# Two-layer decoder trunk on one core: the first three products run together, and each unit of the heads has its scores, turns and output next to each other ahead of one piece of fill

## The chip, the cores and the metric

The kernel runs on one core of one Trainium2 chip. The metric is the device time of one execution in microseconds (us); the time before is the median of three runs. A profiled execution of the same kernel gives the trace that all rows below come from.

The core's engines each work through a queue of their own, in order: TensorE (PE in the profile) does matmuls and transposes, VectorE (DVE), ScalarE (ACT) and GpSimd (POOL) do the elementwise work, and SyncE (SP) issues DMAs. Matmul results go to PSUM, in eight buffers of 512 fp32 columns.

## The reference, cut to what matters

One inference step of a two-layer decoder trunk for 544 tokens: one prompt of 512 and eight samples of 4 each. `D_MODEL` is 1024.

```python
def layer(x, ...):
    h = rmsnorm(x, g_mix)
    z = h @ w_in                       # one projection, split by columns
    u_pool, q_raw, kv_raw, nsa_gate, c_b, c_c, c_x, gate_pool, gate_nsa, gate_conv = split_columns(z)
    y_pool, pool_new = pool_mixer(u_pool, ...)    # windows 2, 4, 8, 16, then a small map
    y_nsa, kv_rows, win_new = nsa_mixer(...)      # compressed, selected and window attention, 8 heads of 64
    y_conv, conv_new = short_conv_mixer(c_b, c_c, c_x, conv_past, conv_w)
    merged = (sigmoid(gate_pool) * (y_pool @ w_br_pool)
              + sigmoid(gate_nsa) * (y_nsa @ w_br_nsa)
              + sigmoid(gate_conv) * (y_conv @ w_br_conv))
    x = x + merged @ w_out
    f, ffn_new = conv_ffn(rmsnorm(x, g_ffn), ...) # (silu(conv3(h @ W_a)) * (h @ W_b)) @ W_down
    return x + f, ...
```

`rmsnorm` divides by the root of the mean square over the 1024 features. After the second layer a final norm gives the two outputs. Everything is fp32.

## The kernel before

**Layout and products.** `x` lies with features on partitions: eight tiles of 128 features by 544 tokens. A product multiplies eight weight tiles of 128x128 into two halves of 272 tokens. Every fp32 operand is split into a high and a low part in the format fp32r, and `mm3` (L328 to L332) does three matmuls for one tile and half: high by high, high by low, low by high. So one half of a product is 24 matmuls of 272 columns. A weight comes by DMA (L312, tile `wr`), ACT casts its high part in two halves (L304, `wh`), and DVE, or POOL while the heads run, subtracts the low part (L305, `wl`).

**The order.** PE's order is written by hand: `emit` runs through a list of products and `pump(us)` asks it for so many microseconds of product matmuls. ACT's and SP's orders are by hand in `setup` only. All other orders (DVE and POOL everywhere, ACT and SP after `setup`) come from the scheduler that builds the program; it may put an instruction that was written later ahead of an earlier one. `later(n, f)` runs `f` when `n` ticks have passed, and a half of a product (or one compression product) ends with a tick.

**Norm rows.** The squares are summed over tiles by ACT and DVE into `acc`. `rstd_sum` has PE sum over partitions (L381, tile `po`), and then runs a chain of twelve small DVE instructions on 5 columns (L384 to L390; three Newton steps of three instructions each, tiles `nv`, `ni`, `ny`, `nt`). `rstd_rows` (L400) broadcasts the result along partitions by transposes, and ACT copies it out of PSUM (L402, L403). The evacuations of the products that follow multiply by it (for instance L506 and L513).

**The start.** `setup` loads `x`, the constants and the first weights. In `emit` the first three products of a norm are special: the first two run together over seven tiles, then over the eighth, and the third one comes after; for the first norm the sum stands at its step 6 and the rows at its step 14 of 16. `setup` also loads cache pages (L486, tile `b`) and `begin` the layer's small tables.

**The projection stage.** A product of pooling inputs is followed, `pm` = 9 and 10 ticks later, by `pool_map` for its two halves: a matmul into a score buffer (L713, tile `ps`), ACT's scaled cast (L714) and DVE's low part (L715). Two groups of 16 tiles make the compressed keys and values: `cmp_split` splits the page rows with eight ACT casts (L566) and eight DVE subtractions (L568), and two compression products (L1383 to L1385) use them. The scores' tag has two PSUM buffers (`PS`), the turns' tag two (`PT`), products three (`G`), and sums and head outputs one (`PO`).

**The heads.** `attention` walks through 64 units a layer: 8 heads, two branches kk (0 selected, 1 window), four blocks b of 128 queries. In what follows S(kk,b) are the scores of a unit (L864), with DVE's causal add (L878), its negated maximum (L880), ACT's exponential (L886), DVE's reciprocal (L891) and POOL's scaling (L893, tile `P`). T(kk,b) is the turn of a unit, b+1 transposes on PE into one `PT` buffer (L906), evacuated by ACT (L908) and DVE (L909). C is the turn of the head's compressed scores (L930), which takes a `PT` buffer too (evacuated by L932 and L933). `head_out` (L939, L944) multiplies by the values. `head_q` makes the next head's scaled queries with two ACT instructions (L849) and two DVE instructions (L851, tile `Q`). Step u emits the scores of unit u, the turn of unit u-3, C when unit u-5 is (0,3), and outputs further back. Between these come pieces of fill, that is product matmuls (tile `pg`) which `yield self.fill / 2` (0.83 us each) asks for.

**The tail.** The last product writes the output tiles (`final_tile`, L1274 to L1285). Rows for the first half of the tokens come from one more chain, `final_rows` (L1295) multiplies by them, and `final_tokens` transposes the rest (L1307), sums `acc` and `side` (L381) and scales (L1318, L1319).

## Time and profile before

| what | value |
|---|---|
| median of three runs | 1736.14 us (1735.8 to 1737.05) |
| profiled execution: time, span | 1735.2 us, 1733.3 us |
| granted clock of the core, mean | 0.997 |
| PE busy | 1709.6 us (99% of the span), 13525 instructions |
| DVE, ACT, POOL busy | 1126.6, 740.4, 468.2 us |
| DMA | 175.52 MB, mean 101 GB/s |

The span is the stretch from the first to the last recorded instruction; 1.9 us lie around it. Busy time is summed over the whole span, so it says little of one stage: the timeline of a stretch shows what each engine did there, and the list of waits shows who stood still for whom. A row of a timeline gives the start and the length in us, the engine, the line of the program, the operation, the tiles as output<-inputs, shapes, the count of merged instructions and, in brackets, how long the engine had stood idle and what released it. PEclk is the granted clock of PE as a share of full speed. Matmuls overlap, so a row's length is longer than the distance from one to the next.

### The profile page before, as it was taken

How to read it: one execution, taken by the hardware profiler on the slowest of the kernel's cores; microseconds unless marked ns; L12 is line 12 of the kernel's file. 1: busy time of each engine (PE TensorE's matmuls, PEld its weight loads, DVE VectorE, ACT ScalarE, POOL GpSimd, SP SyncE). 2: the span in 40 equal slices, each digit the busy share in tenths (PEclk: the TensorE clock that was granted, in tenths of full speed). 3: DMA queues.
4: the chain of work that ended last, by engine and by line, in shares of the span. 5: the costliest groups of instructions: out<-in, count | busy, mean ns of one | idle time of the engine just before them, and what ended most of it. 6: DMA issues, size and time to landing. Idle time of an engine off the chain costs nothing.

```text
span 1733.3 us, 35135 instructions
## 1 busy us (share of the span) xinstructions
PE 1709.6 (99%) x13525; PEld 1689.0 (97%) x13525; DVE 1126.6 (65%) x2572; ACT 740.4 (43%) x1501; POOL 468.2 (27%) x692
## 2 busy tenths in 40 slices
PE   7999999999999999999999999999999999999998
PEld 7999999999999999999999899999999999999997
DVE  5675688756566565565757757877565665565666
ACT  4443566653333232233444436666443433232333
POOL 2412446630122121012034124566101321121120
PEclk9999999999999999999999999999999999999999
DMA  7546212235322322322455532212242222322322
GB/s 215 151 127 199 76 51 60 68 88 173 91 86 69 104 81 84 104 86 71 152 175 117 170 123 62 62 52 66 68 161 90 88 77 89 92 80 81 109 79 76
DMA packets 95976, 175.52 MB, mean 101 GB/s; under 512 B 30898, under 2 KB 49970, under 8 KB 95810
## 3 DMA queue, kind: packets, MB, share of 16 engines
q1 hardware_dynamic: 95666, 173.01, 33.4%
q8 instruction: 107, 1.75, 0.4%
q14 instruction: 59, 0.48, 0.1%
q10 hardware_dynamic: 144, 0.28, 0.1%
HBM read 157.19 MB, written 12.71 MB: 98 GB/s over the span
## 4 chain that ended last, share of the span: by engine, by line
PE 93%; DVE 2%; DMA 1%; ACT 1%; issue 1%; SPq 1%; POOL 1%; DVEq 0%; POOLq 0%; ACTq 0%
PE pg L329 27%; PE pg L330 27%; PE pg L332 27%; PE ps L864 2%; PE po L944 2%; PE pt L906 2%; DVE t L568 1%; PE ps L332 1%; PE ps L330 1%; PE ps L329 1%; DMA W<-W 1%; ACT b L566 1%; PE pt L930 0%; PE ps L1383 0%; PE po L381 0%
## 5 line engine op out<-in xcount | busy, mean ns | idle before, releaser
L329 PE MATMUL pg<-t,wh 128*128 128x272 f32 (+1 forms) x3808 | 1112.8, 293 | 2.1 <-ACT t L1260 1.4
L330 PE MATMUL pg<-t,wh 128*128 128x272 f32 (+1 forms) x3808 | 1095.6, 288 | 1.4 <-DVE t L1261 1.3
L332 PE MATMUL pg<-t,wl 128*128 128x272 f32 x3776 | 1086.5, 288 | 0.0
L329 PEld LDWEIGHTS pg<-t,wh 128*128 128x128 f32 (+1 forms) x3808 | 715.8, 188 | 6.7 <-ACT t L1260 2.0
L330 PEld LDWEIGHTS pg<-t,wh 128*128 128x128 f32 (+1 forms) x3808 | 716.0, 188 | 3.4 <-DVE t L1261 2.2
L332 PEld LDWEIGHTS pg<-t,wl 128*128 128x128 f32 x3776 | 711.0, 188 | 0.0
L304 ACT CAST wh<-wr 128x512 fp32r<-128x512 f32 (+2 forms) x524 | 313.3, 600 | 559.2 <-PE pg L330 438.7
L305 DVE TENSOR_TENSOR wl<-wr,wh 128x512 fp32r<-128x512 f32 (+2 forms) x428 | 290.7, 681 | 169.8 <-ACT wh L304 152.0
L1171 DVE TENSOR_TENSOR t<-t,pg 128x272 f32<-128x272 f32 x204 | 88.8, 436 | 92.8 <-PE pg L332 91.8
L1210 POOL TENSOR_TENSOR W<-W,W 128x512 f32<-128x512 f32 x44 | 77.9, 1770 | 229.2 <-ACT wh L304 190.3
L305 POOL TENSOR_TENSOR wl<-wr,wh 128x512 fp32r<-128x512 f32 (+1 forms) x96 | 113.2, 1183 | 35.9 <-ACT wh L304 33.6
L893 POOL TENSOR_SCALAR P<-P,ls,gate 128x128 f32<-128x128 f32 (+3 forms) x128 | 81.3, 635 | 121.3 <-DVE lc L920 43.2
L650 POOL COPY t<-W 128x2 f32<-128x2 f32 x44 | 10.8, 246 | 358.4 <-DVE W L1193 321.1
L348 DVE TENSOR_TENSOR t<-W,t 128x544 fp32r<-128x544 f32 x48 | 34.9, 727 | 78.5 <-ACT t L347 78.4
L886 ACT ACTIVATE P<-ps,mx 128x256 f32<-128x256 f32 (+1 forms) x144 | 71.7, 499 | 33.0 <-DVE mx L880 23.4
L908 ACT CAST b<-pt 128x128 fp32r<-128x128 f32 (+3 forms) x128 | 54.2, 423 | 71.4 <-PE pt L906 71.0
L909 DVE TENSOR_TENSOR b<-pt,b 128x128 fp32r<-128x128 f32 (+3 forms) x128 | 62.1, 485 | 10.3 <-ACT b L908 8.9
L347 ACT CAST t<-W 128x544 fp32r<-128x544 f32 x48 | 31.1, 647 | 82.8 <-POOL W L1211 78.2
L880 DVE TENSOR_REDUCE mx<-ps 128x1 f32<-128x256 f32 (+1 forms) x144 | 64.4, 447 | 1.6
L864 PE MATMUL ps<-t,Q 128*128 128x288 f32 (+6 forms) x288 | 62.5, 306 | 1.0 <-ACT P L886 0.7
L1200 ACT ACTIVATE W<-W 128x560 f32<-128x560 f32 x44 | 29.6, 673 | 74.8 <-DVE W L640 74.8
L369 POOL TENSOR_TENSOR t<-t,W 128x544 f32<-128x544 f32 x12 | 16.4, 1368 | 154.5 <-ACT W L360 154.5
(266 smaller groups left out, 1856.7 us busy)
## 6 DMA issues: line engine op xcount, KB each, us to landing
wr<-up SPq DMA_DIRECT2D x88, 512.0 KB, 3.6
wr<-w_in SPq DMA_DIRECT2D x82, 512.0 KB, 3.8
wr<-down SPq DMA_DIRECT2D x64, 256.0 KB, 2.7
wr<-w_out SPq DMA_DIRECT2D x16, 512.0 KB, 3.7
wr<-down SPq DMA_DIRECT2D x32, 192.0 KB, 2.4
b<-pgA SPq DMA_DIRECT2D x64, 64.0 KB, 2.5
wr<-cw SPq DMA_DIRECT2D x8, 512.0 KB, 4.7
wr<-br_a SPq DMA_DIRECT2D x32, 128.0 KB, 2.2
```

The source lines that it names most:

```text
L304: nc.scalar.copy(h, r[:, k0:k1])
L305: (eng or nc.vector).tensor_sub(w, r[:, k0:k1], h)
L329: self.nc.tensor.matmul(p[:m, :HF], wh, xh[:, cs], start=a, stop=False)
L330: self.nc.tensor.matmul(p[:m, :HF], wh, xl[:, cs], start=False, stop=b and wl is None)
L332: self.nc.tensor.matmul(p[:m, :HF], wl, xh[:, cs], start=False, stop=b)
L864: nc.tensor.matmul(p[:, :n], q[:, 128 * i:128 * i + 128], kd[:, c0:c0 + n], start=u == 0, stop=u == 1)
L880: nc.vector.tensor_reduce(mx[:, u:u + 1], p[:, c0:c0 + m], axis=AX.X, op=OP.max, negate=True)
L886: nc.scalar.activation(t[:, pos:pos + m], p[:, c0:c0 + m], AF.Exp, bias=mx[:, 0:1], accum_out=ls[:, u:u + 1])
L893: nc.gpsimd.tensor_scalar(t[:, 0:n], t[:, 0:n], ls[:, 0:1], self.gate[:, i, 1 + kk, hd:hd + 1], op0=OP.mult, op1=OP.mult)
L909: nc.vector.tensor_sub(blk(pt)[:, lo][:, ::-1], blk(p)[:, 0:i + 1], blk(pt)[:, hi])
L1171: self.halves(ps, lambda p, cs: nc.vector.tensor_add(self.x[m][:, cs], self.x[m][:, cs], p))
L1210: nc.gpsimd.tensor_mul(f[:, 0:NP], t[:, 0:NP], z[:, 0:NP])
```

## The change

The change touches five places.

1. **Start.** `setup` loads and splits the weights of three products, not two, in parts. For the first norm `emit` runs the three products together, tile by tile (six PSUM buffers), with the partition sum after the seventh tile and the rows after the eighth. Four pages move from `setup` into `begin`.
2. **Chain.** `rstd_sum` has one DVE instruction fewer (the shift by one is folded into a product with -0.5). A second accumulator goes through `token_sums` on its own and is added by one DVE instruction.
3. **Pool maps.** `pm` is 7 instead of 9.
4. **Heads.** `attention` collects the fill of a step and yields once, at its end.
5. **Other norms and tail.** In the other norms the sum comes ahead of the third product and the rows between its halves. In the tail the first `final_rows` come one tick later, two of the four after the last product.

```diff
-    def __init__(... pm=9, ...):
+    def __init__(... pm=7, ...):
...
+    def token_sums(self, p, acc, c0, n):
+        for j in range(-(-n // 128)):
+            t0 = c0 + min(128 * j, n - 128)
+            self.nc.tensor.matmul(p[:, j:j + 1], acc[:, t0:t0 + 128], self.ones[:, 0:1], start=True, stop=True)
+
-    def rstd_sum(self, acc, c0=0, n=NT):
+    def rstd_sum(self, acc, c0=0, n=NT, more=None):
...
+        self.token_sums(p, acc, c0, n)
         nc.vector.tensor_scalar(v, p[:, 0:nb], 1.0 / D, 1e-6, op0=OP.mult, op1=OP.add)
-        nc.vector.tensor_scalar(it, v.bitcast(I32), 1, None, op0=OP.logical_shift_right)
-        nc.vector.tensor_scalar(y.bitcast(I32), it, -1.0, float(0x5f3759df), op0=OP.mult, op1=OP.add)
+        if more is not None:
+            q = p[:, 8:8 + nb]
+            self.token_sums(q, more, c0, n)
+            nc.vector.scalar_tensor_tensor(v, q, 1.0 / D, v, op0=OP.mult, op1=OP.add)
+        nc.vector.tensor_scalar(y.bitcast(I32), v.bitcast(I32), -0.5, float(0x5f3759df), op0=OP.mult, op1=OP.add)
...
         norm(0)
-        part(0, 0, 2)
-        part(1, 0, 2)
+        for n in range(3):
+            part(n, 0, 2)
...
-        self.ahead(3)
...
         self.pages_cmp()
-        self.pages_some(0, range(0, 4))
...
-                yield self.fill / (1 if u < lag else 2)
+                us += self.fill / (1 if u < lag else 2)
             if 0 <= u - lag < len(units):
                 n, kk, b = units[u - lag]
                 self.head_turn(heads[n], kk, b)
-                yield self.fill / 2
+                us += self.fill / 2
             if 0 <= u - lag - 2 < len(units):
                 n, kk, b = units[u - lag - 2]
                 if (kk, b) == (0, 3):
                     self.head_cmp_turn(heads[n])
-                    yield self.fill / 2
+                    us += self.fill / 2
             for d, k1 in ((lag + 4, 0), (lag + 1, 1)):
                 if 0 <= u - d < len(units) and units[u - d][1:] == (k1, 3):
                     self.head_out(heads[units[u - d][0]], k1)
+            yield us
...
-                    for k in range(0, KT, 2):
-                        self.later(4 + k // 2, lambda k=k: self.final_rows(k))
+                    for k in (0, 2):
+                        self.later(5 + k // 2, lambda k=k: self.final_rows(k))
...
+        self.final_rows(4)
+        self.final_rows(6)
         turn(0, range(KT - 1))
-        y = self.rstd_sum([self.acc, self.side], HF, HF)
+        y = self.rstd_sum(self.acc, HF, HF, self.side)
...
+            if n == 0:
+                w3, rs = self.take(2), [self.G(), self.PT()]
+                for k in range(KT):
+                    for p, a, b in ((ps, w, t), (qs, w2, u), (rs, w3, v)):
+                        self.outer(p, a, x, [k], b.m)
+                    if k == KT - 2:
+                        y = self.rstd_sum(self.acc)
+                self.r = self.T()
+                self.rstd_rows(y, self.r)
...
```

Line numbers move by 0 to 8, so L851 is L853 after the change, L864 is L866, L906 is L908, L909 is L911 and L930 is L932. Three places show how the queues stand. In these rows a number behind a tile's name tells one buffer's use from another.

The first place is DVE at the start: the chain of the first norm (tiles `ny`, `nt`) and the low parts `wl` of a weight. Before, from the end of the second Newton step:

```order
L390 SCALAR_TENSOR_TENSOR ny_443<-nt_444,ny_443 128x5
L388 SCALAR_TENSOR_TENSOR nt_444<-ny_443 128x5
L389 TENSOR_TENSOR nt_444<-nt_444,nv_442 128x5
L305 TENSOR_TENSOR wl_298<-wr_295,wh_297 128x512
L390 SCALAR_TENSOR_TENSOR ny_443<-nt_444,ny_443 128x5
L506 TENSOR_TENSOR W_497<-pg_293,t_482 128x272
```

After, in the same place:

```order
L394 SCALAR_TENSOR_TENSOR ny_451<-nt_452,ny_451 128x5
L392 SCALAR_TENSOR_TENSOR nt_452<-ny_451 128x5
L305 TENSOR_TENSOR wl_302<-wr_299,wh_301 128x512
L393 TENSOR_TENSOR nt_452<-nt_452,nv_450 128x5
L305 TENSOR_TENSOR wl_306<-wr_299,wh_305 128x512
L394 SCALAR_TENSOR_TENSOR ny_451<-nt_452,ny_451 128x5
L392 SCALAR_TENSOR_TENSOR nt_452<-ny_451 128x5
L393 TENSOR_TENSOR nt_452<-nt_452,nv_450 128x5
L394 SCALAR_TENSOR_TENSOR ny_451<-nt_452,ny_451 128x5
L508 TENSOR_TENSOR W_499<-pg_297,t_487 128x272
```

One low part stood inside the chain, ahead of its last step; now two halves of one weight do, with four steps behind the second.

The second place is the first compression split of a layer on DVE. Before, three of its eight subtractions (b_217 to t) with what stands ahead and behind; five like them are left out:

```order
L723 TENSOR_TENSOR W_1415<-pg_1387,W_1415 24x272
L543 TENSOR_TENSOR t_1409<-pt_1404,t_1409 128x4x64
L724 TENSOR_TENSOR W_1415<-W_1415,t_482 24x272
L568 TENSOR_TENSOR t_1508<-b_217,b_1506 128x326
...
L568 TENSOR_TENSOR t_1526<-b_217,b_1506 128x326
L543 TENSOR_TENSOR t_1412<-pt_1404,t_1412 128x4x64
L568 TENSOR_TENSOR t_1529<-b_217,b_1506 128x326
L506 TENSOR_TENSOR W_1493<-pg_1433,t_482 128x272
L305 TENSOR_TENSOR wl_1363<-wr_1360,wh_1362 128x512
```

After:

```order
L726 TENSOR_TENSOR W_1417<-W_1417,t_487 24x272
L545 TENSOR_TENSOR t_1414<-pt_1406,t_1414 128x4x64
L508 TENSOR_TENSOR W_1505<-pg_1435,t_487 128x272
L717 SCALAR_TENSOR_TENSOR t_1461<-ps_1462,t_234,t_1460 128x272
L570 TENSOR_TENSOR t_1520<-b_221,b_1518 128x326
...
L570 TENSOR_TENSOR t_1541<-b_221,b_1518 128x326
L305 TENSOR_TENSOR wl_1365<-wr_1362,wh_1364 128x512
```

A product's evacuation (L508, of pg_1435) and a pool map's low part (L717) went ahead of the split. On ACT, the second split's casts (b_1691) and the next weights before:

```order
L304 CAST wh_1362<-wr_1360 128x512
L304 CAST wh_1366<-wr_1360 128x512
L566 CAST b_1691<-b_218 128x326 x8
L304 CAST wh_1425<-wr_1423 128x512
L304 CAST wh_1429<-wr_1423 128x512
L714 ACTIVATE t_1556<-ps_1558,t_274 128x272
```

After:

```order
L716 ACTIVATE t_1460<-ps_1462,t_234 128x272
L304 CAST wh_1364<-wr_1362 128x512
L304 CAST wh_1368<-wr_1362 128x512
L716 ACTIVATE t_1460<-ps_1491,t_234 128x272
L568 CAST b_1693<-b_222 128x326 x8
L304 CAST wh_1427<-wr_1425 128x512
```

Both pool maps (L714, now L716) stand ahead of the casts; the weight casts behind them keep their place.

The third place is the end of a head on PE, here the second head of the first layer: S(1,3) into ps_3373, T(1,0) into pt_3391, the next head's S(0,0) into ps_3401, T(1,1) into pt_3423, C into pt_3434; the product matmuls between them are left out. Before:

```order
L864 MATMUL ps_3373<-t_708,Q_2922 128x512
L864 MATMUL ps_3373<-t_708,Q_2923 128x512
...
L906 MATMUL pt_3391<-cst,P_3252 128x128
...
L864 MATMUL ps_3401<-t_594,Q_3287 128x160
L864 MATMUL ps_3401<-t_594,Q_3288 128x160
...
L906 MATMUL pt_3423<-cst,P_3281 128x128 x2
...
L930 MATMUL pt_3434<-cst,cm_2928 32x128 x4
```

After, with ps_3375, pt_3387, ps_3403, pt_3415 and pt_3420 for the same things:

```order
L866 MATMUL ps_3375<-t_710,Q_2924 128x512
L866 MATMUL ps_3375<-t_710,Q_2925 128x512
L908 MATMUL pt_3387<-cst,P_3254 128x128
...
L866 MATMUL ps_3403<-t_596,Q_3289 128x160
L866 MATMUL ps_3403<-t_596,Q_3290 128x160
L908 MATMUL pt_3415<-cst,P_3283 128x128 x2
L932 MATMUL pt_3420<-cst,cm_2930 32x128 x4
```

Between S(1,3) and C stood 27 product matmuls (6, 6, 9 and 6), and now 12 in one piece. At the other heads' ends it is 27 or 30 before and 15 after, 21 and 15 at the last one. DVE before, from the evacuation of the turn T(0,3) ahead of S(1,3):

```order
L909 TENSOR_TENSOR b_3220<-pt_3348,b_3220 128x4x128
L891 RECIPROCAL ls_3334<-ls_3334 128x1
L878 TENSOR_TENSOR ps_3373<-ps_3373,cst 128x128
L880 TENSOR_REDUCE mx_3376<-ps_3373 128x1
L851 SCALAR_TENSOR_TENSOR Q_3655<-t_877,Q_3654 64x512 x2
L909 TENSOR_TENSOR b_3390<-pt_3391,b_3390 128x128
```

After, in the same place:

```order
L911 TENSOR_TENSOR b_3216<-pt_3343,b_3216 128x4x128
L1141 SCALAR_TENSOR_TENSOR t_3111<-t_3111,pg_3353 128x272
L893 RECIPROCAL ls_3336<-ls_3336 128x1
L880 TENSOR_TENSOR ps_3375<-ps_3375,cst 128x128
L882 TENSOR_REDUCE mx_3378<-ps_3375 128x1
L853 SCALAR_TENSOR_TENSOR Q_3657<-t_879,Q_3656 64x512 x2
L911 TENSOR_TENSOR b_3386<-pt_3387,b_3386 128x128
```

The evacuation of T(1,0) (b_3390, now b_3386) stands behind the next head's two Q instructions in both; only the evacuation of T(0,3) is one product's evacuation further ahead.

## Rows read from the trace of the kernel before

**Rows 1.** The page, part 1: busy us (share of the span) x instructions.

```profile
PE 1709.6 (99%) x13525; PEld 1689.0 (97%) x13525; DVE 1126.6 (65%) x2572; ACT 740.4 (43%) x1501; POOL 468.2 (27%) x692
```

**Rows 2.** Waits of PE: engine, line, waited for; us in total, times, longest.

```profile
PE po L400 <- issue: 4.8, 1, 4.8
PE ps L713 <- DVE t L715: 3.3, 2, 1.7
PE ps L1383 <- DVE t L715: 1.2, 2, 0.6
```

**Rows 3.** Timeline, PE, start: start us, us, engine, line, operation, count, idle.

```profile
34.27 1.09 PE L400 MATMUL po<-cst,ny 128*128 128x128 f32 x4 [4.80 <-issue]
```

**Rows 4.** Timeline, DVE, start.

```profile
33.40 0.69 DVE L305 TENSOR_TENSOR wl<-wr,wh 128x512 fp32r<-128x512 f32 x1 [4.72 <-ACT wh L304]
34.01 0.16 DVE L390 SCALAR_TENSOR_TENSOR ny<-nt,ny 128x5 f32<-128x5 f32 x1
```

**Rows 5.** Timeline, ACT, start.

```profile
32.75 0.62 ACT L304 CAST wh<-wr 128x512 fp32r<-128x512 f32 x1 [9.64 <-DMA wr<-w_in]
```

**Rows 6.** Stretches, start: us, engines' busy us, PEclk, DMA share, GB/s.

```profile
33.00:36.00 3.00, 1.73 (x8) 1.69 (x8) 0.77 (x2) 0.97 (x3) 0.00 (x0) 0.50 0.53 121
```

**Rows 7.** Timeline, PE, first layer, around the compression products.

```profile
98.75 0.37 PE L329 MATMUL pg<-t,wh 128*128 128x272 f32 x1
115.56 0.72 PE L713 MATMUL ps<-W,t 128*128 128x272 f32 x2 [1.58 <-DVE t L715]
122.88 0.42 PE L1383 MATMUL ps<-b,wh 128*128 128x324 f32 x1 [0.60 <-DVE t L715]
```

**Rows 8.** Timeline, DVE, same stretch: the eight subtractions of a split, twice.

```profile
101.05 5.04 DVE L568 TENSOR_TENSOR t<-b,b 128x326 fp32r<-128x326 f32 x7
106.34 0.76 DVE L568 TENSOR_TENSOR t<-b,b 128x326 fp32r<-128x326 f32 x1
115.43 5.72 DVE L568 TENSOR_TENSOR t<-b,b 128x326 fp32r<-128x326 f32 x8
```

**Rows 9.** Timeline, ACT, same stretch: a split's casts, then a weight's.

```profile
107.14 5.89 ACT L566 CAST b<-b 128x326 fp32r<-128x326 f32 x8 [1.55 <-DVE t L568]
112.91 1.16 ACT L304 CAST wh<-wr 128x512 fp32r<-128x512 f32 x2
```

**Rows 10.** Timeline, PE, one head's end: S(1,3), the next fill matmul, C.

```profile
273.65 0.62 PE L864 MATMUL ps<-t,Q 128*128 128x512 f32 x2
274.11 0.29 PE L329 MATMUL pg<-t,wh 128*128 128x272 f32 x1
278.63 0.61 PE L930 MATMUL pt<-cst,cm 128*32 128x128 f32 x4
```

**Rows 11.** Timeline, DVE: an earlier Q, then the stretch of rows 10.

```profile
206.75 1.37 DVE L851 SCALAR_TENSOR_TENSOR Q<-t,Q 64x512 fp32r<-64x512 f32 x2
...
274.50 0.28 DVE L878 TENSOR_TENSOR ps<-ps,cst 128x128 f32<-128x128 f32 x1
275.54 2.72 DVE L851 SCALAR_TENSOR_TENSOR Q<-t,Q 64x512 fp32r<-64x512 f32 x2
278.28 0.29 DVE L909 TENSOR_TENSOR b<-pt,b 128x128 fp32r<-128x128 f32 x1
```

**Rows 12.** Instructions of line L930: what PE waited for ahead of them (us, times).

```profile
  DVE b L909: 1.0, 4
```

**Rows 13.** Groups, DVE, 200 to 330 us: line, shapes, count, busy us, mean ns.

```profile
L851 DVE SCALAR_TENSOR_TENSOR Q<-t,Q 64x512 fp32r<-64x512 f32 x12 | 12.1, 1012 | 0.2
```

**Rows 14.** Timeline, POOL, the stretch of rows 10.

```profile
275.98 1.72 POOL L305 TENSOR_TENSOR wl<-wr,wh 128x512 fp32r<-128x512 f32 x1
```

**Rows 15.** Timeline, PE, the norm rows near the end.

```profile
1715.32 0.51 PE L400 MATMUL po<-cst,ny 128*128 128x128 f32 x3 [1.08 <-DVE ny L390]
```

**Rows 16.** Timeline, DVE, near the end.

```profile
1719.25 1.73 DVE L1295 SCALAR_TENSOR_TENSOR W<-t,norms,t 128x272 f32<-128x272 f32 x4
1724.39 0.16 DVE L384 TENSOR_SCALAR nv<-po 128x3 f32<-128x3 f32 x1 [1.65 <-PE po L381]
```

More of the change, by code (lines that the diff above doesn't have):

```diff
@@ L377, in rstd_sum @@
         nb = -(-n // 128)
-        for j in range(nb):
-            t0 = c0 + min(128 * j, n - 128)
-            for u, a in enumerate(acc):
-                nc.tensor.matmul(p[:, j:j + 1], a[:, t0:t0 + 128], self.ones[:, 0:1], start=u == 0, stop=u == len(acc) - 1)
         v, y, t = self.S(nb, "nv"), self.S(nb, "ny"), self.S(nb, "nt")
-        it = self.S(nb, "ni", I32)
+        self.token_sums(p, acc, c0, n)
         nc.vector.tensor_scalar(v, p[:, 0:nb], 1.0 / D, 1e-6, op0=OP.mult, op1=OP.add)
-        nc.vector.tensor_scalar(it, v.bitcast(I32), 1, None, op0=OP.logical_shift_right)
-        nc.vector.tensor_scalar(y.bitcast(I32), it, -1.0, float(0x5f3759df), op0=OP.mult, op1=OP.add)
+        if more is not None:
[3 more added lines that the diff above has]
+        nc.vector.tensor_scalar(y.bitcast(I32), v.bitcast(I32), -0.5, float(0x5f3759df), op0=OP.mult, op1=OP.add)
         for _ in range(3):
@@ L426, in setup @@
         nc.gpsimd.memset(self.cT[64:128].bitcast(F32), 0.0)
-        ap = [self.tl[n].w[0] for n in range(2)]
-        raw = [self.raw_weights(8) for _ in range(2)]
+        ap = [self.tl[n].w[0] for n in range(3)]
+        raw = [self.raw_weights(8) for _ in range(3)]
         load = lambda n, k0, k1: nc.sync.dma_start(raw[n][:, k0:k1], ap[n][:, k0:k1])
@@ L443, in part @@
             if k0 % 4 == 0:
-                tiles[n] = [self.wp.tile([128, NP], F32R, tag=t, name=self.nm("w" + t[0])) for t in ("hi", "lo")]
+                tiles[n] = [self.T(NP, F32R) if n == 2 else self.wp.tile([128, NP], F32R, tag=t, name=self.nm("w" + t[0]))
+                            for t in ("hi", "lo")]
             a, b = (t.rearrange("p (a b) -> p a b", b=128)[:, k0 % 4:k0 % 4 + k1 - k0] for t in tiles[n])
@@ L450, in setup @@
         norm(0)
-        part(0, 0, 2)
-        part(1, 0, 2)
+        for n in range(3):
+            part(n, 0, 2)
         norm(1)
-        part(0, 2, 4)
-        part(1, 2, 4)
+        for n in range(3):
+            part(n, 2, 4)
         norm(2)
         norm(3)
-        part(0, 4, 8)
-        part(1, 4, 8)
-        self.nxt = 2
+        for n in range(3):
+            part(n, 4, 8)
+        self.nxt = 3
         for k in range(4, KT):
             norm(k)
-            if k > 4:
-                square(k - 5)
-        self.ahead(3)
+            square(k - 4)
         nc.sync.dma_start(self.cst, i["cst"])
         nc.sync.dma_start(self.ptt, i["pt"])
-        for k in range(3, KT):
+        for k in range(4, KT):
             square(k)
         self.pages_cmp()
-        self.pages_some(0, range(0, 4))
     def page(self, j):
@@ L972, in attention @@
         for u in range(len(units) + lag + 3):
+            us = 0.0
             if u < len(units):
@@ L1034, in begin @@
                 nc.sync.dma_start(t, i["rope"][u])
+            if l == 0:
+                self.pages_some(0, range(0, 4))
         def raw_kv(j):
@@ L1401, in emit @@
             qs = [self.PS(), self.PS()]
-            for ks in (range(KT - 1), range(KT - 1, KT)):
-                self.outer(ps, w, x, ks, t.m)
-                self.outer(qs, w2, x, ks, u.m)
-            self.tick()
-            w3, rs = self.take(n + 2), [self.G(), self.PT()]
-            at = (6, 14) if n == 0 else (0, 8)
-            step = 0
-            for hf in range(2):
-                for _ in self.half(rs[hf], hf, w3, x, v.m):
-                    if step == at[0]:
-                        y = self.rstd_sum([self.acc])
-                    if step == at[1]:
+            if n == 0:
[7 more added lines that the diff above has]
+                self.rstd_rows(y, self.r)
+            else:
+                for ks in (range(KT - 1), range(KT - 1, KT)):
+                    self.outer(ps, w, x, ks, t.m)
+                    self.outer(qs, w2, x, ks, u.m)
+                self.tick()
+                w3, rs = self.take(n + 2), [self.G(), self.PT()]
+                y = self.rstd_sum(self.acc)
+                for hf in range(2):
+                    for _ in self.half(rs[hf], hf, w3, x, v.m):
+                        pass
+                    if hf == 0:
                         self.r = self.T()
                         self.rstd_rows(y, self.r)
-                    step += 1
             for a, p in ((t, ps), (u, qs), (v, rs)):
```

7 lines of the change are left out of this document (3 added, 4 removed).

## The prediction

> **What bounds the kernel now.** I read the page's engine table first: the reader is to see that TensorE (PE) is busy for 1709.6 of 1733.3 us [rows 1], so nothing that is done off PE is worth time unless PE waits for it; 1709.6 us over 13525 matmuls gives 0.126 us as the price of one. Then the list of PE's waits: the dear ones are the norm rows of the start (L400, 4.8 us) and two that end with DVE's L715 (3.3 and 1.2 us, each from two places) [rows 2]. All that a change can win is in these few waits; all that it can lose is a new wait or a dearer matmul. Then I read the stretch around each wait, engine by engine, to see what stood ahead of the late instruction. The profiled execution took 1735.2 us, 0.9 below the median of the runs (1736.14); I add to 1735.2 and put the 0.9 on at the end.
>
> **1. The first three products (gain sought: the 4.8 us wait).** PE stands until 34.27, when the norm rows start [rows 3]. They need the last step of the rstd chain, DVE's L390 at 34.01, and that step stands in DVE's queue behind a weight's low part (L305, 33.40) [rows 4], which needs ACT's cast at 32.75, which had idled 9.64 us until the weight's DMA landed [rows 5]. So the wait is one for a weight's landing, not for the first products. The change does the products sooner, but leaves the chain on the same queue, and in the order after two low parts of that weight stand inside the chain, with four chain steps behind the second one, instead of one low part with one step behind it. Landing to chain's end: 1.4 us before (32.75 to 34.17); after it is cast 0.6, cast 0.6, subtraction 0.6 to 0.7 and four steps at about 0.2 each (a step is 0.16 us in [rows 4, 16]), about 3 us. The weight may land a little sooner, as four of the page loads are now issued behind it, or later, as one more weight is read ahead of it: my estimate is -0.7 to +0.5 us around 32.75. Rows therefore at about 35.0 to 36.2. PE has less left to do behind the rows, since the rest of the third product now lies ahead of them, but the next product takes PSUM buffers that are free only when ACT and DVE have used the rows, so nothing of that is won. I take **+1.3 us** (0 to +2.5). After the wait PE's granted clock was 0.50, its lower level (1.2 GHz), for at least the 3 us from 33 to 36 [rows 6]; a wait of the same kind stands there after the change, so I cost the clock at no difference.
>
> **2. The pool maps two ticks sooner (gain sought: 4.5 us).** A pool map is a PE matmul, then ACT, then DVE's L715, and takes one of two score buffers. In the first layer PE waits 1.58 us for it at 115.56 and 0.60 at 122.88 [rows 7]; the second layer has the same two waits ([rows 2] has all four). The L715s are late since they stand on DVE near the eight subtractions of a compression split (L568, 5.0 us for seven at 101.05, the eighth at 106.34, eight more in 5.72 us from 115.43 [rows 8]). The change puts the maps between the halves of an earlier product, so PE waits no more for an L715. But DVE's order moves too: ahead of the first split now stand a product's evacuation (L508) and one map's L717, which can't run before the half is through on PE: 24 matmuls from 98.75 [rows 7] end at about 101.8, then a map, ACT and DVE, so the split starts at about 103.5 instead of 101.05, an estimate, and ends 2.1 later, at 109.2. The second split's eight casts on ACT wait for its end (107.14 before, right behind the 106.34 + 0.76 of [rows 8]) and take 5.89 us; the casts of the next product's weight stand behind them on ACT (112.91 before [rows 9]). They move to about 115.0, and their low parts to about 116.4. PE, freed of the map, wants this weight at about 114.4: it waits some 2 us there and about 0.5 us for the second half of the weight. The new wait takes the place of the old: **0** for both layers (-4.5 if the weight is in time, +1 if the split slides further).
>
> **3. The heads: one piece of fill per unit.** Per layer there are 64 units. Joining the small products saves at most a little at transitions; PE's fill has the same number of matmuls. I take **-0.7** (-2 to 0). What matters is the turns' two PSUM buffers. The turn of the compressed scores (C, L930) takes the buffer of the turn of unit (1,0) of the same head, since one other turn lies between them, and must wait until DVE has evacuated that (L909). DVE runs this L909 behind the next head's two L851 (tile Q), and these behind the mask and the maximum of the head's last scores, S(1,3). At 273.65 S(1,3) starts on PE, and C starts at 278.63 [rows 10]; the two L851 take 2.72 us from 275.54, L909 follows at 278.28 and ends at 278.57 [rows 11], 0.06 us ahead of C. C already waits for this L909 four times, 1.0 us in all over both layers [rows 12]. There is no slack, and the change takes C nearer: between S(1,3) and C stand 27 or 30 fill matmuls before, and 12 or 15 after; 5 of the 6 places of a layer that have a next Q in the way lose 15 (1.9 us), one 12 (1.5 us). C then is due, from the start of S(1,3): 0.46 for that (273.65 to the next row at 274.11), 15 x 0.126 of fill, and some 0.45 (an estimate by their columns) for the one transpose, the next scores and two transposes between them: 2.8 us (2.4 where it is 12). The evacuation ends 4.92 us after that start (278.57 minus 273.65), with an L851 pair of 2.72. The twelve L851 of one layer's six places take 12.1 us, 2.02 a pair [rows 13], so at the mean place the evacuation ends 4.92 - 0.70 = 4.2 us after the start. With five places at 2.8 and one at 2.4 C is due at 2.7, and waits 1.5 us, six times: 9 us a layer, less the 0.5 that is paid now. One thing helps: DVE's evacuation of the turn before that, 0.6 to 0.7 us, is done one fill piece sooner, and no longer in the way of mask and maximum; at 273.65 this can give 0.2 (DVE begins at 274.50, S(1,3) is through at 274.27), and I give it 0.3 at each place, 1.8 us a layer. So 6.6 a layer, **+13 us** for both. The ends: if every pair takes 1.37 as at 206.75 and DVE begins when S(1,3) is through, the evacuation ends 0.62 + 1.04 (274.50 to 275.54) + 1.37 + 0.3 = 3.3 us after the start, and the waits are 0.6 at six places less 0.5, +6 for both layers; if DVE gains nothing, +17. Behind the waiting C on PE stands all the fill, and nothing else is fed; ACT and POOL only idle longer. The turns' own inputs, POOL's scaled scores, were there microseconds before.
>
> Two L851 took 1.37 us where POOL did nothing with wide tiles, and 2.72 where POOL's low part (L305, 1.72 us) ran from 275.98 [rows 11, 14]. The Trainium skill, SBUF — State Buffer, section Who interferes with whom, says that a VectorE instruction with two SBUF inputs and a GpSimd instruction that reads SBUF block each other, one waiting for the whole of the other. The two durations agree with it. By that rule the price would hang on where POOL's subtractions fall in the new order: a rival below is the case in which they miss Q.
>
> **4. The other two norms.** The rows there have half a microsecond of slack, the sum and the rows move by the same 3 matmuls, and the chain is one step shorter: 0.
>
> **5. The tail.** PE waits 1.08 us at 1715.32 for the chain [rows 15]; 12 matmuls later, with a chain one step (0.2 us) shorter, it does not. Four of the row products (L1295, 1.73 us at 1719.25) now stand ahead of the last chain, which started at 1724.39 [rows 16], but they leave the place that they had ahead of the final tiles, and the last tile comes sooner by the wait. I take **-1.3** (-1.0 to -1.6).
>
> **Sum.** 1735.2 + 1.3 + 0 + 13 - 0.7 - 1.3 = 1747.5, and with the 0.9 to the median 1748.4; I forecast 1748.
>
> **Rivals.**
> - *A, the forecast*: C waits for the slot. 1748, 1741 to 1754 by the ends above without their extremes.
> - *B, Q runs free of POOL*: the twelve pairs take 1.37 each, the heads cost 6 and not 13: about 1741, and 1738 to 1744 with the start's bounds. For it: the pair at 206.75 took that [rows 11]. Against: the mean pair took 2.02 [rows 13], and POOL's work is the same amount.
> - *C, faster*: C is not held up, because DVE has evacuated (1,0) within 2.7 us of the start of S(1,3), and the maps' waits go. 1736.1 + 1.3 - 4.5 - 0.7 - 1.3 = 1731. For it: the change takes DVE work out of the way. Against: the best case that I can build from rows is 3.3 us; it decides at 2.7, where C is due.
> - *D, the start does what its shape says*: the chain ends before the weights land, so the 4.8 us go; with the heads' 13 about 1742. Against: the steps stand behind the low parts on an in-order engine.
> - *E, worse*: heads +17, start +2.5, z +1: 1756.
>
> **How the numbers follow.** Chances: A 0.61, B 0.14, C 0.12, D 0.07, E 0.06. A measurement of this kernel can tell about 0.2 %, 3.5 us, from no change. Faster by more (under 1732.7): most of C, 0.10. Within: the rest of C, the lower half of B and the low ends of A and D, 0.15. Slower: 0.75. The range for 8 in 10 leaves out most of C and the top of E: 1734 to 1755.
>
> **What would show it.** PE's waits after: C (L932) waiting for L911 about twelve times at 1 to 2 us each; no wait for L717 but one for a cast or low part of the product behind the second split, near 114 to 116 and in the second layer alike; one wait of 6 to 8 us for the norm rows that ends at 35 to 36; none at the tail's rows. I am wrong if C's line has less than 5 us of waits, or if the rows of the start come before 33.

## The result, and the profile after

The changed kernel takes 1752.72 us (median; 1751.69 to 1752.76), the one before 1735.97 in the same comparison: 1.0097 times as long, with a 95% interval of 1.0084 to 1.0110. It is 16.8 us slower, where 12 were forecast. The profiled execution has a span of 1750.8 us against 1733.3, so 17.5 us more; PE is busy 1711.4 us against 1709.6 [rows 1], so nearly all of it is waiting.

PE's list of waits after the change (engine, line, what it waited for: us in total, times, longest):

```profile
PE pt L932 <- DVE b L911: 15.6, 12, 2.1
PE po L404 <- issue: 6.7, 1, 6.7
PE po L376 <- DVE t L369: 2.5, 1, 2.5
PE pt L748 <- issue: 1.8, 2, 1.0
...
PE po L376 <- DVE nv L385: 1.0, 1, 1.0
```

The first line is new and is the story: C (L930 before, L932 now) waits at twelve places for the evacuation of T(1,0). The waits for the pool maps' low part (L715), which stood in [rows 2] at the pool map's matmul (L713) and at the compression product (L1383), are gone. The wait for the norm rows of the start is longer (6.7 for 4.8) and has another of 2.5 us ahead of it.

To see where the 17.5 us arise I took, from PE's timelines of both kernels, the times of the same instructions:

| instruction on PE | before | after | difference | added in this stage |
|---|---|---|---|---|
| norm rows of the start | 34.27 | 35.95 | +1.68 | +1.68 |
| first scores, layer 1 | 187.93 | 189.32 | +1.39 | -0.29 projection stage |
| rows of the second norm | 486.50 | 495.67 | +9.17 | **+7.78** heads and what follows them |
| rows of the third norm | 885.18 | 894.77 | +9.59 | +0.42 |
| first scores, layer 2 | 1037.38 | 1047.13 | +9.75 | +0.16 projection stage |
| rows of the fourth norm | 1336.12 | 1355.35 | +19.23 | **+9.48** heads |
| rows of the last norm | 1715.32 | 1734.12 | +18.80 | -0.43 |
| last transposes | 1725.23 | 1743.13 | +17.90 | -0.90 |

One caution on the two bold numbers: after the change the rows of a norm inside the layers stand three matmuls (3 x 0.126 = 0.4 us) earlier in PE's order. heads_undone, below, has the same order as the changed kernel everywhere but in the heads. Against it the two heads stages are 8.23 and 9.82 us longer, 18.05 in all and not 17.3.

The heads' ends show it at work. PE, at the fifth head's end of the first layer in the changed kernel (start, length, engine, line, tiles, shapes, count, idle and releaser):

```profile
302.60 0.63 PE L866 MATMUL ps<-t,Q 128*128 128x512 f32 x2
303.07 0.27 PE L908 MATMUL pt<-cst,P 128*128 128x128 f32 x1
...
305.07 0.35 PE L866 MATMUL ps<-t,Q 128*128 128x160 f32 x2
305.26 0.39 PE L908 MATMUL pt<-cst,P 128*128 128x128 f32 x2
307.71 0.61 PE L932 MATMUL pt<-cst,cm 128*32 128x128 f32 x4 [2.06 <-DVE b L911]
```

DVE, same stretch:

```profile
302.57 0.69 DVE L911 TENSOR_TENSOR b<-pt,b 128x512 fp32r<-128x512 f32 x1
...
303.60 0.28 DVE L880 TENSOR_TENSOR ps<-ps,cst 128x128 f32<-128x128 f32 x1
303.92 0.69 DVE L882 TENSOR_REDUCE mx<-ps 128x1 f32<-128x512 f32 x1
304.52 2.81 DVE L853 SCALAR_TENSOR_TENSOR Q<-t,Q 64x512 fp32r<-64x512 f32 x2
307.36 0.29 DVE L911 TENSOR_TENSOR b<-pt,b 128x128 fp32r<-128x128 f32 x1
```

POOL, same stretch:

```profile
303.75 1.29 POOL L305 TENSOR_TENSOR wl<-wr,wh 128x512 fp32r<-128x512 f32 x1 [1.35 <-ACT wh L304]
305.01 1.78 POOL L1149 TENSOR_TENSOR t<-t,W 128x544 f32<-128x544 f32 x1
```

These answer to [rows 10, 11, 14], which show the fourth head's end before. S(1,3) starts at 302.60; T(1,0), a piece of fill, the next head's scores and T(1,1) follow, and PE is through with them at 305.65. DVE masks and takes the maximum, then runs the two Q instructions (L853), 2.81 us for 1.37 when alone, while POOL runs two wide operations, and only then evacuates T(1,0) at 307.36. C starts at 307.71, 2.06 us late by the row.

### The profile page after: what moved, and what is told of

Same layout as the page of the kernel before. It is cut to its first block, busy times and chain, and to the rows that moved or that the text cites. A ratio compares the mean times of both kernels' runs of the same rounds, so it can differ in the third digit from the quotient of the medians.

```text
span 1750.8 us, 35104 instructions
## 1 busy us (share of the span) xinstructions
PE 1711.4 (98%) x13525; PEld 1688.7 (96%) x13525; DVE 1140.5 (65%) x2568; ACT 747.9 (43%) x1502; POOL 467.9 (27%) x692
## 4 chain that ended last, share of the span: by engine, by line
PE 91%; DVE 4%; ACT 2%; DMA 1%; issue 1%; SPq 0%; DVEq 0%; ACTq 0%
PE pg L329 27%; PE pg L330 27%; PE pg L332 26%; PE po L946 2%; PE ps L866 2%; PE pt L908 2%; DVE Q L853 1%; DVE t L570 1%; PE ps L330 1%; PE ps L332 1%; PE ps L329 1%; PE pt L932 1%; ACT b L568 0%; DMA wr<-w_in 0%; ACT Q L851 0%
## 5 line engine op out<-in xcount | busy, mean ns | idle before, releaser
L911 DVE TENSOR_TENSOR b<-pt,b 128x128 fp32r<-128x128 f32 (+3 forms) x128 | 61.9, 483 | 5.2 <-ACT b L910 3.7
L866 PE MATMUL ps<-t,Q 128*128 128x288 f32 (+6 forms) x288 | 62.8, 307 | 1.1 <-ACT P L888 1.1
```

The lines of the kernel that those rows point to most:

```text
L866: nc.tensor.matmul(p[:, :n], q[:, 128 * i:128 * i + 128], kd[:, c0:c0 + n], start=u == 0, stop=u == 1)
L911: nc.vector.tensor_sub(blk(pt)[:, lo][:, ::-1], blk(p)[:, 0:i + 1], blk(pt)[:, hi])
```

## The experiments

My theory: the loss is C's wait for its PSUM slot, held by T(1,0) until DVE has passed Q. The rivals: joining the products is dear by itself, the start or the pool maps cost the time, or the evacuation is late for another reason. All ratios are against the kernel before in the same comparison. "c_late" is a base for the smaller terms, since C's waits are out of the way there.

### The heads undone, and alone

heads_undone puts the pieces of fill back, in the changed kernel:

```diff
-                us += self.fill / (1 if u < lag else 2)
+                yield self.fill / (1 if u < lag else 2)
...
-                us += self.fill / 2
+                yield self.fill / 2
...
-            yield us
```

> The changed kernel with the three pieces of fill per unit of the heads put back, all else as changed. Slot theory (the loss is C's wait for the PSUM buffer of T(1,0), which DVE evacuates behind the next head's two Q instructions): C waits as little as before (under 1 us in all), the 16 to 17 us of the heads go, about 1736 us. Rival, the loss is elsewhere (start, norms, projection stage): over 1745 us.

Measured: 1735.05 us, ratio 0.9992 (0.9983 to 1.0002): no difference from before can be told. The line of C is gone from the list of waits, and the first line now is the start's:

```profile
PE po L404 <- issue: 6.9, 1, 6.9
```

So the four other parts together cost nothing measurable, and the loss needs the joined units.

heads_alone makes that edit, the other way round, in the kernel before and changes nothing else.

> The kernel before with nothing but the one yield per unit. Slot theory: C waits 15 to 16 us at twelve places, about 1752 us. Rival, the loss needs the other parts too (shorter chain, pool maps, other start): under 1745 us.

Measured: 1754.79 us, ratio 1.0100 (1.0083 to 1.0117), even a little more than the whole change. C's line in its list of waits:

```profile
PE pt L930 <- DVE b L909: 15.7, 12, 2.1
...
PE ps L713 <- DVE t L715: 3.1, 2, 1.6
```

The same twelve waits, 15.7 us. The joined units are sufficient, and the pool maps' waits (L713) are those of before. This profile loses more than the changed kernel does: its two heads stages are 9.8 and 11.2 us longer than before. PE's granted clock fell behind three of the twelve waits here, and behind one in the changed kernel; what that costs is worked out further down.

### C one unit later

```diff
-            if 0 <= u - lag - 2 < len(units):
-                n, kk, b = units[u - lag - 2]
+            if 0 <= u - lag - 3 < len(units):
+                n, kk, b = units[u - lag - 3]
```

> The changed kernel with C one unit later, behind T(1,2): it then takes the buffer of T(1,1), and T(1,2) takes that of T(1,0), 12 to 15 fill matmuls (1.5 to 1.9 us) later than C did. Slot theory: waits of 0.6 to 2.1 us shrink to 0.3 at the most at each place, under 2 us in all, about 1737 us (1735 to 1741). Rival, joining the products is dear by itself (dearer transitions, one long piece of fill starves DVE and then PE): about 1752 us as now. Rival, the new place only moves the wait to T(1,2) or to the output: 1745 us or more.

Measured: 1734.05 us, ratio 0.9986 (0.9976 to 0.9996). The joined units stay joined; only the slot that C asks for, and when the held one is asked for, is another. The waits for L911 are gone from the list (here the first line and the last one):

```profile
PE po L404 <- issue: 5.1, 1, 5.1
...
PE pt L908 <- POOL P L895: 0.2, 1, 0.2
```

The time is 1 us below the expected band. This kills the rival that joining is dear by itself. Nor does joining gain anything that can be told, against the 0.7 I had put down: from the first scores to the norm's rows behind the heads c_late takes 298.06 and 298.39 us in the two layers, and heads_undone, with the same other parts and separate pieces of fill, 298.12 and 298.40.

### Half a piece of fill ahead of C

```diff
                 if (kk, b) == (0, 3):
+                    yield self.fill / 2
                     self.head_cmp_turn(heads[n])
-                    us += self.fill / 2
```

> The changed kernel with a piece of fill of half size (9 or 10 matmuls, 1.2 us) put back between T(1,1) and C alone, and the fill behind the unit that much smaller. Slot theory gives a dose: every wait of C shrinks by the 1.2 us that it comes later, so of 0.64, 1.03, 0.76, 1.49, 2.06 and 1.83 us in each layer 0, 0, 0, 0.3, 0.9 and 0.6 are left, 3 to 4 us in all instead of 15.6, and the time is 1737 to 1741 us. Rival, joined scores and turns are what costs: 1750 us or more.

Measured: 1740.96 us, ratio 1.0027 (1.0018 to 1.0037). PE's waits:

```profile
PE pt L932 <- DVE b L911: 6.3, 6, 1.3
```

and the three of the first layer in PE's timeline:

```profile
279.93 0.61 PE L932 MATMUL pt<-cst,cm 128*32 128x128 f32 x4 [0.74 <-DVE b L911]
...
304.50 0.61 PE L932 MATMUL pt<-cst,cm 128*32 128x128 f32 x4 [1.30 <-DVE b L911]
...
328.82 0.61 PE L932 MATMUL pt<-cst,cm 128*32 128x128 f32 x4 [1.10 <-DVE b L911]
```

The time falls in the expected band, and six waits are left, as expected, but of 0.74, 1.30 and 1.10 us and not 0.3, 0.9 and 0.6. In the changed kernel these three were 1.49, 2.06 and 1.83: each fell by 0.73 to 0.76. At these places the piece holds six matmuls (6 x 0.126 = 0.76 us) and not the nine of the second and third head's ends on which I had worked out 1.2. So the dose comes out: what C comes later is what it waits less, within 0.03 us.

### Q's low parts on POOL

```diff
-        for c in (a, b):
-            nc.vector.scalar_tensor_tensor(ql[c], src, 0.125, qh[a], op0=OP.mult, op1=OP.subtract)
+        qs = self.S(256, "qs")
+        for s in (slice(0, 256), slice(256, 512)):
+            nc.gpsimd.tensor_scalar(qs[a], src[:, s], 0.125, None, op0=OP.mult)
+            for c in (a, b):
+                nc.gpsimd.tensor_sub(ql[c, s], qs[a], qh[a, s])
```

> The changed kernel with the next head's Q low parts on POOL (two halves, each a scaling and two subtractions) and not on DVE. Theory that Q is what holds the evacuation: it ends 2 us sooner, 2.0 to 2.4 us after the start of S(1,3), ahead of C at 2.7, so C's waits fall from 15.6 to under 3 us; the time is 1737 to 1742, since POOL may be late with Q for the next head's scores. Rival, the evacuation is late for another reason (mask, maximum, the turn's own cast): C's waits stay over 8 us.

Measured: 1739.98 us, ratio 1.0019 (1.0009 to 1.0028). C waits nowhere; there are new waits elsewhere:

```profile
PE pg L329 <- DVE W L508: 3.8, 2, 2.4
PE ps L869 <- ACT P L891: 3.5, 7, 1.0
```

The evacuation of T(1,0) now ends 2.2 to 2.8 us after the start of S(1,3), where it took 3.4 to 5.1 in the changed kernel. So Q on DVE was what held it. As a remedy it ends 6 us behind c_late, but most of that isn't in the heads: the two waits for L508 lie in the projection stages of the two layers (2.4 us at 95.84, 1.4 in the second layer), and up to the first scores these stages take 3.3 and 1.7 us more than in c_late. The heads stages, where PE waits for ACT's exponential (L891) at seven places, take 0.3 and 1.7 more.

### The start

Three edits on c_late. cl_start_undone has the start of before (two products together, two weights in parts, the pages in `setup`; the edit is the change's own part 1, reversed). DVE's order, which the scheduler makes, did not come out as it was before: no low part stands inside the chain here.

> The changed kernel with C one unit later (as in c_late, so that the heads' waits are out of the way) and the start as it was before the change: two products together, the third behind them, four pages in the setup. Theory of the prediction (the start of the change costs about 1.3 us, as two low parts cut the chain and the low clock lasts longer): PE's wait for the rows falls from 5 to 7 us to under 5 us, the rows start at about 34.3, and the time falls by 1 to 3 us against c_late, to about 1732 us. Rival, the change's start is worth its lost wait: 1736 us or more.

Measured: 1733.57 us, ratio 0.9982 (0.9973 to 0.9991), against 0.9986 for c_late: the two intervals overlap. In the profiles the first scores come at 187.42, and at 188.87 in c_late: 1.45 us less. As the chain runs whole in this kernel, that is the price against a start with an uncut chain, not against the start of before. The mechanism that I named is not all of it, since the rows start at 28.94 here, not at about 34.3, and PE then waits for the evacuation instead:

```profile
28.94 0.60 PE L404 MATMUL po<-cst,ny 128*128 128x128 f32 x4
...
34.50 0.39 PE L329 MATMUL pg<-t,wh 128*128 128x272 f32 x1 [4.48 <-DVE W L510]
```

cl_chain_whole has the low parts of the fourth and fifth weight on POOL:

```diff
-                self.got[self.nxt] = self.weights(*t.w, t.m, self.nc.gpsimd if self.busy else None, t.keep is not None)
+                self.got[self.nxt] = self.weights(*t.w, t.m, self.nc.gpsimd if self.busy or self.nxt in (4, 5) else None, t.keep is not None)
```

> c_late with the low parts of the fourth and fifth product's weights on POOL, so that DVE's chain of the first norm is not cut. Theory that the low parts in the chain set the rows: the chain ends at about 28.5 instead of 35.9 and the rows start on PE then; but ACT's copy of the rows still stands behind two casts of the weight that lands at about 33, and ends near 35, so the next product starts at about 35.5 instead of 38.1 and the time falls by 2 to 3 us, to about 1731. Rival, the rows wait for something else (the DMA of constants, the sum): the rows stay at 35 or later, 1734.

Measured: 1733.25 us, ratio 0.9984 (0.9975 to 0.9993), 0.8 us below c_late's median, 0.3 by the ratios, and not the 2 to 3 expected. The rows come at 27.98 instead of 36.05, so the low parts in the chain did set them. The gain is lost to the next in line, PE first and then ACT in the same stretch:

```profile
27.98 0.62 PE L404 MATMUL po<-cst,ny 128*128 128x128 f32 x4
...
35.24 0.59 PE L329 MATMUL pg<-t,wh 128*128 128x272 f32 x1 [6.54 <-ACT W L515]
```

```profile
33.19 1.14 ACT L304 CAST wh<-wr 128x512 fp32r<-128x512 f32 x2 [10.94 <-DMA wr<-w_in]
34.24 0.58 ACT L406 COPY t<-po 128x512 f32<-128x512 f32 x1
...
35.07 0.41 ACT L515 COPY W<-pt 128x272 f32<-128x272 f32 x1
```

ACT's copy of the rows (L406) stands behind the casts of the weight that lands at 33.19. The next product starts at 35.24, as expected, 2.9 us sooner than in c_late (38.19), but the first scores only 0.56 us sooner.

cl_later_casts loads these weights as early, and casts them after the rows' copies:

```diff
+            if self.held is not None:
+                r = self.raw_weights(t.w[1], t.m)
+                self.nc.sync.dma_start(r, t.w[0])
+                self.held.append((self.nxt, r, t))
...
+                held, self.held = self.held, None
+                with self.tc.manual_schedule(engines={mybir.EngineType.Activation}):
+                    self.rstd_rows(y, self.r)
+                    for j, r, a in held:
+                        self.got[j] = [p for k0 in (0, 4) for p in self.weight_parts(r, k0, k0 + 4)]
```

> c_late with the fourth and fifth product's weights loaded as early as now, but cast and subtracted only after the rows' copies on ACT. If the chain and the copies are all that the fourth product waits for, it starts at about 30.5 instead of 38.1, the wait for the rows falls under 2 us, and the time falls by 5 to 8 us, to about 1728. Rival: PE then waits for these weights or for the tables of the evacuation, and the gain is under 3 us (1731 to 1734).

Measured: 1732.34 us, ratio 0.9982 (0.9972 to 0.9991), the lowest time of all, though the interval overlaps those of c_late and of the two runs before. The next product now starts at 31.62, 6.6 us sooner than in c_late, and yet the first scores come only 1.04 us sooner. The rival is what happened. PE's largest wait, and its waits for low parts:

```profile
PE pg L329 <- DVE W L679: 3.3, 1, 3.3
...
PE pg L332 <- DVE wl L305: 2.6, 6, 1.1
```

and DVE's rows ahead of the largest:

```profile
61.02 0.72 DVE L521 TENSOR_TENSOR t<-t,W 128x544 f32<-128x544 f32 x1 [4.72 <-POOL W L676]
61.66 0.43 DVE L679 TENSOR_TENSOR W<-pg,t 128x272 f32<-128x272 f32 x1
```

PE, ahead by 6 us, runs into the pool products' evacuation (L679), which stands on DVE behind an instruction that waits 4.72 us for POOL, and POOL in its turn had stood 6.71 us for a DMA:

```profile
59.65 1.33 POOL L520 TENSOR_TENSOR W<-W,t 128x544 f32<-128x544 f32 x1 [6.71 <-DMA W<-W]
```

Behind PE's wait its granted clock is 0.54 from 63 to 66, which costs time too. In this kernel the wait at the start covers for a stage behind it that is not ready sooner.

### The pool maps

cl_pm9 is c_late with `pm` back at 9.

> c_late with the pool maps two ticks later, as before the change (pm 9). Term of the prediction: 0 for both layers. By it the waits for DVE's L717 come back (4 to 5 us) and those at L748 and for the weight behind the second split go (3 us): 1733 to 1736 us. Rival, the sooner pool maps win their 4.5 us: 1738 us or more. Rival, the new order costs: 1732 us or less.

Measured: 1739.56 us, ratio 1.0016 (1.0007 to 1.0025), 5 us more than c_late, which spoke against my 0. So I did the step alone in the kernel before, pm_alone: `pm` 7 and nothing else.

> The kernel before with the pool maps two ticks sooner and nothing else. The term of the prediction: no difference (1735 to 1737 us), PE's waits for L715 (4.5 us) replaced by ones at the gates' transposes and at the weight behind the second split. Rival, from the run with the maps two ticks later on top of the change, which was 5 us slower than its counterpart: 3 us or more faster, 1733 us or less.

Measured: 1735.02 us, ratio 0.9993 (0.9984 to 1.0002): nothing that can be told. From PE's list of waits of pm_alone:

```profile
PE pt L746 <- issue: 1.8, 2, 0.9
...
PE pg L332 <- DVE wl L305: 1.2, 5, 0.3
```

L713's and L1383's waits for L715 [rows 2] are gone, and these have come. The 5 us of cl_pm9 are another matter: in the second layer it differs from c_late by 0.1 us over the projection stage. In the first it loses 1.2 us between the compression products and the first scores, and 3.5 us ahead of them, from the rows on, in one place that c_late doesn't have (PE, then two stretches of 3 us: busy us, PEclk, DMA share, GB/s):

```profile
94.35 0.39 PE L329 MATMUL pg<-t,wh 128*128 128x272 f32 x1 [1.95 <-DVE W L508]
```

```profile
94.00:97.00 3.00, 2.65 (x15) 2.65 (x16) 2.84 (x11) 0.54 (x1) 0.28 (x2) 0.72 0.94 280
97.00:100.00 3.00, 3.00 (x18) 2.87 (x18) 1.56 (x4) 1.01 (x3) 0.21 (x1) 0.71 0.40 123
```

One product waits 1.95 us for an evacuation that the scheduler had put on DVE behind a small weight's subtraction (L324, which itself stood 3.94 us for ACT's cast) and two more instructions; in c_late it stands ahead of that subtraction. PE's granted clock then was 0.72 and 0.71 for 6 us. So what two ticks are worth depends on the order that the scheduler makes around them: 5 us in that kernel, nothing that can be told in the kernel before.

## Why the prediction was right, and where its sizes were off

The sum forecast 12.3 us for the profiled execution; its span grew by 17.5, and the last transposes came 17.9 later.

**The start, +1.3: right in its mechanism, and in size in part by luck.** The rows came at 35.95, in the band of 35.0 to 36.2, and for the reason given. ACT and DVE in the changed kernel, answering to [rows 4, 5]:

```profile
33.16 1.14 ACT L304 CAST wh<-wr 128x512 fp32r<-128x512 f32 x2 [10.60 <-DMA wr<-w_in]
37.08 0.59 ACT L406 COPY t<-po 128x512 f32<-128x512 f32 x1 [2.78 <-PE po L404]
```

```profile
33.81 0.69 DVE L305 TENSOR_TENSOR wl<-wr,wh 128x512 fp32r<-128x512 f32 x1 [6.58 <-ACT wh L304]
...
34.49 0.69 DVE L305 TENSOR_TENSOR wl<-wr,wh 128x512 fp32r<-128x512 f32 x1
...
35.69 0.17 DVE L394 SCALAR_TENSOR_TENSOR ny<-nt,ny 128x5 f32<-128x5 f32 x1
```

The weight landed at 33.16 and the chain ended 2.7 us later (forecast about 3). From the start of the weight's cast to the rows it is 2.79 us here, 2.79 or 2.80 in the five other kernels with the changed start, and 1.52 before (32.75 to 34.27). The landing itself moves more than that from one execution to another: heads_alone and pm_alone, with the start of before, have the cast at 31.51 and 34.40 and the rows at 33.03 and 35.92, again 1.52 later. So the 1.3 us of the cut chain are shown, and that this one pair of traces gives +1.68 is in part chance. Two things were not seen. The sum now waits 2.5 us for the squares. And the low clock, which I costed at no difference, lasts longer (granted clock in the last column but two):

```profile
27.00:30.00 3.00, 2.27 (x11) 1.95 (x9) 0.20 (x2) 0.00 (x0) 0.65 (x2) 0.51 0.98 300
...
39.00:42.00 3.00, 3.00 (x15) 3.00 (x15) 2.03 (x2) 0.00 (x0) 2.92 (x5) 0.50 0.86 209
42.00:45.00 3.00, 3.00 (x18) 3.00 (x17) 0.00 (x0) 0.39 (x1) 2.28 (x6) 0.65 0.86 306
```

It is at its lower level (0.50, 1.2 GHz) from 27 to 42 and mostly so to 45, where before it was back at 0.89 from 39 to 42; PE had stood for 2.5 us until 24.69 first, then worked on small sums and a few matmuls, and then stood again. Between the rows and the compression products the changed kernel loses 1.02 us more, and the projection stage gives 1.31 back. The step "the rows are what the next product waits for" was too simple: the runs on the start show that with the rows 6 to 8 us sooner 0.6 to 1.5 us are left at the first scores.

**The pool maps, 0: right, but made up otherwise.** In the second layer's projection stage, where the start has no part, the difference is 0.16 us. The split's slide was there: its first subtraction starts at 105.22 (forecast 103.5, and the rows were 1.7 us late), and the weight behind the second split's casts is cast from 116.71 (forecast 115.0). PE's new waits are at the gates' transposes, which I hadn't named, and at the casts and low parts behind the second split, which I had:

```profile
112.76 0.59 PE L748 MATMUL pt<-gt,t 32*128 32x24 f32 x4 [0.89 <-issue]
...
117.38 0.39 PE L329 MATMUL pg<-t,wh 128*128 128x272 f32 x1 [0.24 <-ACT wh L304]
...
118.10 0.39 PE L332 MATMUL pg<-t,wl 128*128 128x272 f32 x1 [0.21 <-DVE wl L305]
...
120.10 0.39 PE L332 MATMUL pg<-t,wl 128*128 128x272 f32 x1 [0.24 <-DVE wl L305]
```

The waits behind the second split are 0.7 us a layer and not the 2.5 of the forecast, and the 0.9 at the gates' transposes were not in the sum.

**The heads, +13 and -0.7: right in cause, 5 us too small.** Forecast were twelve waits of 1 to 2 us; the rows give 15.6 us in twelve, of 0.64 to 2.06. The stages lost 17.3 us (7.78 + 9.48) against the kernel before, and 18.05 against heads_undone. What these 18.05 are made of:
- The waits are 15.6 us, and my terms give 14 (13 and the 1.0 which I thought was paid before). Two places of a layer, not one, have 12 matmuls in the way (the second and the third head's end), and the relief of 0.3 us a place wasn't there: the evacuation ended on average 4.2 us after the start of S(1,3), as in the mean I had before taking it off. Against that, C was due later than I had it, 3.05 us after that start with 15 matmuls in the way and 2.65 with 12, not 2.8 and 2.4. And the 1.0 of [rows 12] was read wrongly: that view counts the weight load and the matmul apart. It says 34.0 us, 24 times, for the changed kernel, where the list of waits says 15.6 and 12; for the kernel before, the list has no wait of C at all.
- A wait costs more than its row: from the start of the matmul before C to the start of C, the six places of the first layer make 8.75 us beyond the usual 0.11, and 7.8 in the rows. A row counts the idle time from the end of the matmul before, about 0.27 us after its start, where C otherwise starts 0.11 after that start. That is 0.16 us a place, 1.9 in all. By the same measure the four places of the kernel before, and of heads_undone, were worth 0.2 each, 0.8 in all.
- After the last of the second layer's waits the clock fell, which I had not thought of (columns as above):

```profile
1189.00:1192.00 3.00, 1.46 (x9) 1.43 (x10) 2.61 (x8) 0.89 (x4) 1.39 (x2) 0.83 0.00 0
1192.00:1195.00 3.00, 3.00 (x17) 3.00 (x17) 1.02 (x3) 0.31 (x3) 0.45 (x1) 0.60 0.03 5
```

  That head took 3.24 us longer than before, and its like in the first layer, with the same wait of 1.83 us and a clock of 1.00 behind it, 1.82: so 1.4 us. In heads_alone the three heads whose clock fell were 1.6 us longer each than their like in the changed kernel where it stayed at 1.00.
- Joining gained nothing that can be told, by c_late and heads_undone; the -0.7 of the sum is shown by no run.

That is 15.6 + 1.9 - 0.8 + 1.4 = 18.1, for the 18.05 that the landmarks show. Whether Q meets POOL mattered less than I allowed: the six pairs of the first layer took 1.43 to 2.81 us, 2.12 on average (2.02 before [rows 13]). Q's length did order the places: the shortest waits stand where the pair took 1.4 to 1.7, the longest where it took 2.4 to 2.8. The fifth head's rows above have 2.81 us with POOL busy all through. In the trace of the kernel before, pairs beside which POOL ran nothing took 1.37 to 1.39 (at 63.32, 206.75 and 912.16). In the changed kernel the three places of each layer where POOL's two-input L1149 ran beside the second L853 took 2.44 to 2.81. The rule of the Trainium skill (SBUF — State Buffer, section Who interferes with whom) agrees with these rows; no run here changes POOL's work alone.

**The other norms, 0, and the tail, -1.3: right.** The norms between make 0.42 us, the tail -1.33, and at the last norm's rows no wait is left that answers to [rows 15]; the last chain has a new one of 1.0 us for its second sum (L376 for `nv`), inside that figure.

The rivals that fell: C (no wait) by the list of waits, B (Q free of POOL) by the pairs' 2.12 us on average, D by the start's row. Of E the heads' +17 came nearly true, in part by a clock that it had not counted; its start and pool-map terms did not come. E's terms were also summed wrongly: with the forecast's -0.7 and -1.3 they give 1754.6 and not 1756.

## What to carry to other kernels

With two PSUM buffers in turn, each small product asks for the buffer of the last but one, so the distance from a product to the next but one, in matmuls, has to cover the evacuating engine's whole queue in between. Moving products together takes the fill out of that distance even where each of them was ready, and the cheap remedy was here to change which slot the late one asks for, not to speed up the engine. A long wait near the start need not be a loss of its length: take it away in a run and look at a landmark a stage later before you pay for it.

## What the runs showed of the hardware that I had not expected

PE's clock fell in the middle of dense work too. In the changed kernel the granted clock was 0.83 and 0.60 over 6 us behind one wait of 1.83 us, which made that wait cost 3.2. In heads_alone it fell behind three of the twelve waits (1.86, 2.06 and 1.84 us): 0.63 from 332 to 335, 0.61 from 1165 to 1168, 0.66 from 1192 to 1195. In cl_pm9 it was 0.72 and 0.71 around a wait of 1.95. The changed kernel's three other waits of 1.83 to 2.06 us left it at 1.00, and so did one of 2.41 us in q_pool. What decides between them no run here shows.

## The version to keep

cl_later_casts (the change with C one unit later, and two weights cast after the rows' copies) beats both kernels, the one before by 0.2%: 1732.34 us, 0.9982 of it (0.9972 to 0.9991). Most of this is in c_late, two lines of source, at 0.9986 (0.9976 to 0.9996); the intervals overlap, so that the later casts add anything is not shown.
